# First projection of a two-layer decoder trunk: transposes of the normalised heads issued two half-products later, and the block sums of the second round's left operand formed when its rows are transposed

## Chip, cores and metric

The kernel runs on one core of a Trainium2 chip. The metric is device time in microseconds, the median of three runs. One more execution was taken by the hardware profiler, and all rows of the trace come from it. The engines are called as the profile calls them: PE (matmuls and transposes), PEld (its weight loads), DVE, ACT, POOL, and SP, which in this kernel issues every DMA.

## What is computed

The whole reference is two decoder layers over 2048 positions of width 1024. Only the first step of the first layer matters here: a row-wise RMS norm of x, one projection h @ w_in whose columns are cut into heads, and an RMS norm of the query and key heads of the forgetting attention.

```python
def even_layer(x, g_norm, w_in, b_f, g_q, g_k, w_out):
    h = rmsnorm(x, g_norm)
    proj = h @ w_in
    fq, fk, fv, f_logit, sq, sk, sv, gate = jnp.split(proj, split_points(EVEN_SIZES), axis=-1)
    ...
    fq = rmsnorm(split_heads(fq, N_FOX_HEADS, DENSE_HEAD_DIM), g_q)
    fk = rmsnorm(split_heads(fk, N_FOX_HEADS, DENSE_HEAD_DIM), g_k)
    fox = forgetting_attention(fq, fk, split_heads(fv, N_FOX_HEADS, DENSE_HEAD_DIM), log_f)
```

## The kernel before

The order of the program is: the first projection (`even_projection`, up to about 720 us), the attentions of the first layer, its output projection, and the second layer. Only the first projection is edited.

**Products.** Each fp32 operand is split into a high part (rounded by ACT, line 81) and the remainder (a subtraction on DVE or POOL, line 86), and each product is three matmuls (lines 91 to 93). A panel is 512 output columns for 1024 rows of x. It is computed by a Strassen-like scheme: the left operand (rows of x, transposed) and the weights are 2 by 2 block matrices, seven products A11, S2, A12, S3, S1, A22, S4 (line 177) take the place of eight, and each product is issued as two half-products. A half-product ends with a call of `tick()`, line 292. Four results come out of each panel, after the products A12, S1, A22 and S4; a result is two tiles `c` of 128x512 from the pool tag `res`, which has four buffers. `Weights.prepare` (lines 219 to 245) forms the sums of the weight blocks on POOL (line 226) and splits them into the tiles `wop`.

**Rounds and panels.** The 2048 rows are two rounds of 1024. Each round runs through the panels sq, sk, sv, fv, fk, fq, g0, g1 (line 708). In round 0 the first three are interleaved with the preparation of the left operand straight from x (`left_direct`).

**Heads of fk and fq.** The function `qk_fox` (line 629) takes a result of two tiles, squares them on ACT into tiles `sq` of the tag `c` (line 123; that tag has four buffers), reduces on DVE (line 124), takes an inverse root by short operations on DVE and ACT (lines 104 to 114), scales the tile (line 637), transposes it on PE (line 642), splits it (lines 77, 78) and stores it (line 647). All of this is issued in the program right behind the product.

**Left operand of round 1.** While round 0 runs fv and fk, rows 1024 to 2047 of x are loaded in eight tiles, normalised, transposed and stored to the DRAM array `hT0` (`transpose_to`, line 153, its transposes in line 142 and its copies into tiles `te`, tag `c`, in line 149). The jobs are started at line 743 and advance one step at every second half-product, three tiles in flight (`Pace`, `staggered`). In the last panel of round 0, g1, `left` (line 342) makes the seven blocks: it reloads `hT0` (two loads of 1 MB into `stage`, 16 of 256 KB into `lp`), forms the sums S2, S3, S1, S4 with 20 additions and subtractions of 128x512, half on DVE and half on POOL (line 345), and splits the 28 pieces (ACT line 81, DVE line 86). It advances one step after each product of g1.

**Order.** The order on each engine isn't the order of the program. A scheduler that works on a modelled timeline fixes it ahead of the run: each engine takes, among what is ready by its model, what stands first in the program. Each engine then works off its list in order.

Of the kernel before, what the change touches and what calls it, by code (L numbers as in the profile page):

```python
# [8 lines left out]
F32 = mybir.dt.float32  # L9
F32R = mybir.dt.float32r  # L10
BF = mybir.dt.bfloat16
AF = mybir.ActivationFunctionType
OP = mybir.AluOpType
# [4 lines left out]
P = 128  # L18
S = 2048
D = 1024  # L20
KT = D // P
CH = 512
NCH = S // CH
TPC = CH // P
NTT = S // P
# [11 lines left out]
class K:  # L37
# [114 lines left out]

    def transpose_to(self, T, src, t, gain):

        nc = self.nc
        x = self.w4([P, D], name="xt")
        nc.sync.dma_start(x, src[t * P:(t + 1) * P, :])
        yield
        self.normalise(x)
        yield  # L160
        self.transposed(x, gain, lambda z: self.c2([P, 4, P], name="te"),
                        lambda z, d: nc.sync.dma_start(T[:, z * 4:(z + 1) * 4, t * P:(t + 1) * P], d))

# [12 lines left out]
A11, A12, S2, S3, S1, A22, S4 = range(7)  # L176
ORDER = (A11, S2, A12, S3, S1, A22, S4)
FIRST = (A11, A12, S2, S3, S1, A22, S4)
# [77 lines left out]
def panel(*args, **kw):  # L256
    for _ in panel_steps(*args, **kw):
        pass
# [82 lines left out]

def left(k, T, r, A, staged=True):

# [15 lines left out]
    def piece(block, kk):  # L359
        c = k.c2(name="lp", tag=next(tags))  # L360
        t0 = r * ROUND + block * CH
        nc.sync.dma_start(c, T[:, kk, t0:t0 + CH])
        return c

    half = lambda t, kk: [t[:, kk, z].bitcast(F32) for z in range(2)]
    if staged:
        F = k.big([P, KT, CH], name="stage")
        for z in range(2):
            nc.sync.dma_start(F[:, z * 4:(z + 1) * 4], T[:, z * 4:(z + 1) * 4, r * ROUND:r * ROUND + CH])
    for z, name in enumerate(("A11", "A12")):  # L370
# [48 lines left out]
    yield  # L419


def left_direct(k, x, gain, A, spare):

    nc = k.nc
    sub, plus = OP.subtract, OP.add  # L430
    tt = lambda o, a, b, op, e=None: (e or nc.vector).tensor_tensor(o, a, b, op=op)
    xa, xb = (k.big([P, TPC, D], name=n) for n in ("xa", "xb"))
    tiles = [xa[:, t] for t in range(TPC)] + [xb[:, t] for t in range(TPC)]

    def load(ts):
        for t in ts:
            nc.sync.dma_start(tiles[t], x[t * P:(t + 1) * P, :])

    load(range(1))
    gb = k.w4([P, D], name="gb")  # L440
    nc.sync.dma_start(gb, gain.to_broadcast([P, D]))
    load(range(1, TPC))
    yield
    load(range(TPC, 2 * TPC))
    fa, fb = (k.big([P, KT, CH], name=n) for n in ("fa", "fb"))
    spare.extend(fb[:, j].bitcast(F32R) for j in range(4, KT))
    A.extend([None] * 7)
    new = lambda *js: [A.__setitem__(j, k.big([P, 4, 2, CH], F32R, name=f"A{j}")) for j in js]
    new(A11, A12, S2, A22)
    roots = {}  # L450

    def squares(*ts):
        ss = k.small.tile([P, 8], F32, name="ssx", tag="ss4")
        for j, t in enumerate(ts):
            nc.scalar.activation(k.c2([P, D], BF, name="junk"), tiles[t], AF.Square, accum_out=ss[:, j:j + 1])
        r = k.rstd(ss, 8, D, len(ts))
        for j, t in enumerate(ts):
            roots[t] = r[:, j:j + 1]

    def scaled(t):  # L460
        nc.vector.scalar_tensor_tensor(tiles[t], tiles[t], roots[t], gb, op0=OP.mult, op1=OP.mult)

    def transposed(t):
        pts = []
        for z in range(2):
            pt = k.ps("t" if z else "s")
            for j in range(4):
                c = z * 4 + j
                nc.tensor.transpose(pt[:, j * P:(j + 1) * P], tiles[t][:, c * P:(c + 1) * P], k.ident)
            pts.append(pt.rearrange("p (a b) -> p a b", a=4))  # L470
        return pts

    def put(j, i, src):
        k.split(A[j][:, :, 0, i], A[j][:, :, 1, i], src, "act", "dve")

    squares(0)
    ahead = {0: (1,), 1: (2, 3), 3: (4, 5), 5: (6, 7)}
    for t in range(2 * TPC):
        scaled(t)
        if t in ahead:  # L480
            squares(*ahead[t])
        i = slice(t % TPC * P, (t % TPC + 1) * P)
        p0, p1 = transposed(t)
        if t < TPC:
            for z, j in enumerate((A11, A12)):
                put(j, i, (p0, p1)[z])
                nc.scalar.activation(fa[:, z * 4:(z + 1) * 4, i], (p0, p1)[z], AF.Copy)
            if t == TPC - 1:
                yield
            continue  # L490
        a, s1 = fa[:, :4, i], fb[:, :4, i]
        nc.scalar.activation(s1, p0, AF.Copy)
        tt(a, a, p0, sub)
        s = k.c2([P, 4, P], name="s2")
        tt(s, p1, a, sub)
        put(S2, i, s)
        put(A22, i, p1)
        tt(s1, p1, s1, plus)
        tt(fa[:, 4:, i], fa[:, 4:, i], s, sub, nc.gpsimd)
        yield  # L500
    for j, src in ((S3, fa[:, :4]), (S1, fb[:, :4]), (S4, fa[:, 4:])):
        new(j)
        for kk in range(4):
            k.split(A[j][:, kk, 0], A[j][:, kk, 1], src[:, kk], "act", "dve")
        yield
# [88 lines left out]
def staggered(gens):  # L594

    gens, flight = iter(gens), []
    while True:
        flight = [g for g in flight if next(g, "end") != "end"]
        g = next(gens, None)
        if g is not None:  # L600
            next(g)
            flight.insert(0, g)
        elif not flight:
            return
        yield


def even_projection(k, x, w, first, first_left, early, late):
    tc, nc = k.tc, k.nc
    c2, dr = k.c2, k.dram  # L610
    k.fT = {n: dr.tile([P, 4, 2, S], F32R, name=f"f{n}T") for n in "qk"}
    k.sT = {n: dr.tile([P, 4, 2, S], F32R, name=f"s{n}T") for n in "qk"}
# [1 line left out]
    k.gT = dr.tile([P, 8, S], F32, name="gT")  # L614
    k.ncum = dr.tile([4, S], F32, name="ncum")
    k.mixT = dr.tile([P, 8, S], F32, name="mixT")
    T = dr.tile([P, KT, S], F32, name="hT0")
    y = k.consts.tile([P, 4, 32], F32, name="y")
    nc.gpsimd.memset(y, 0.0)
    r = 0  # L620
    ring, turn = [None], [0]

    def spare():
        turn[0] += 1
        return ring[0][turn[0] % len(ring[0])]
# [3 lines left out]
    def qk_fox(dst, gain):  # L629
        def emit(block, half, cs):  # L630
            rs = k.norms(cs, 4, P)
            for g, src in enumerate(cs):
                one(block, half, g, src, rs[:, g])

        def one(block, half, g, src, rs):
            qn = src.rearrange("p (a b) -> p a b", a=4)
            nc.vector.tensor_tensor(qn, qn, rs.unsqueeze(2).to_broadcast([P, 4, P]), op=OP.mult)
            pt = k.ps("t")
            for pr in range(2):
                for h in range(2):  # L640
                    c = (h * 2 + pr) * P
                    nc.tensor.transpose(pt[:, c:c + P], qn[:, pr * 2 + h], k.ident)
            hl = [spare(), spare()]
            k.split(hl[0], hl[1], pt, scale=getattr(k, gain))
            t0 = at(block, g, 256)
            for z in range(2):
                nc.sync.dma_start(dst[:, half * 2:half * 2 + 2, z, t0:t0 + 256].bitcast(F32),
                                  hl[z].rearrange("p (h t) -> p h t", h=2).bitcast(F32))
        return emit

    def value(dst, logits=False):
# [32 lines left out]
    def forget():  # L684
# [26 lines left out]
        ("sv", plain(2564), "t", value(k.v["s"])),  # L711
        ("fv", [[(1024, 256), (1536, 2)], [(1280, 256), (1538, 2)]], "t", value(k.v["f"], True)),
        ("fk", plain(512), "t", qk_fox(k.fT["k"], "gk")),
        ("fq", plain(0), "t", qk_fox(k.fT["q"], "gq")),
        ("g0", plain(3076), "d", gate(0)),
        ("g1", plain(3588), "d", gate(4)),
    ]
    W = Weights(k, [(w, seg) for _ in range(2) for _, seg, _, _ in kinds], [3] + [1] * 13)
    W.ahead(1)
    next(first)  # L720
    A = first_left
# [4 lines left out]
    tags = ("u", "x", "x")  # L726
# [4 lines left out]
    pace.finish()  # L731
    tick = Pace()
    tick.every = 2
    for r in range(2):
        B = []
        nxt = left(k, T, 1, B)
        box = k.big([P, KT, CH], F32R, name="ring")
        ring[0] = [box[:, j] for j in range(KT)]
        if r == 1:
            k.table()  # L740
        for n, (name, seg, mode, emit) in enumerate(kinds):
            if r == 0 and name == "fv":
                tick.add(staggered(k.transpose_to(T, x, t, k.ge) for t in range(TPC * 2, NTT)))
            if r == 0 and n < len(opened):
                next(opened[n], None)
                continue
            last = r == 0 and name == "g1"
            panel(k, A, W, mode, emit, tick, (lambda j: next(nxt)) if last else None,
                  258 if name == "fv" else 256)
            if r == 1 and name == "fv":  # L750
                forget()
        A = B
# [622 lines left out]
```

## Time and profile before

| | |
|---|---|
| median of 3 runs | 2784.57 us (2783.5 to 2787.73) |
| the profiled execution | 2782.93 us, of which the span from first to last instruction is 2781.2 us |
| busy in the span | PE 96%, DVE 70%, ACT 57%, POOL 40% |
| chain that ended last | PE 72%, DVE 17%, ACT 4%, DMA 3% |
| hT0 stores and reloads | 16 of 256 KB; 2 of 1 MB and 16 of 256 KB |

The page's busy share of PE is made of matmuls that overlap in a pipeline, so it hides lost time; the number of matmuls that start in a stretch shows it better. The view by windows gives both, for any stretch, together with the granted clock of PE. The view of waits says whose end an idle engine waited for. Rows of the timeline are: start, duration, engine, line, operation, output and inputs, count, and in brackets the idle time before it.

### The profile page before, as it was taken

What the parts mean: (1) busy time and instruction counts of PE and PEld (TensorE: products, weight loads), DVE (VectorE), ACT (ScalarE), POOL (GpSimd) and SP (SyncE); (2) the same over time, 40 slices, a digit from 0 to 9 for tenths busy, and PEclk for the clock granted to TensorE, in tenths of its full rate; (3) what the DMA queues carried; (4) which work ended last, traced back from release to release, by engine and by line L of the source; (5) the groups of instructions that cost most, each with busy time, mean ns of one, the idle gap of its engine ahead of it and who ended that gap; (6) DMA issues with size and microseconds to landing.
All of it is one profiled execution on the core that took longest, in us unless ns stands there. A gap on an engine that the chain in (4) does not pass through costs nothing.

```text
span 2781.2 us, 53979 instructions
## 1 busy us (share of the span) xinstructions
PE 2672.4 (96%) x19615; PEld 2423.1 (87%) x19615; DVE 1935.3 (70%) x4257; ACT 1579.9 (57%) x3843; POOL 1105.8 (40%) x905
## 2 busy tenths in 40 slices
PE   6999999999999999999999999999989999999998
PEld 5898878998777789988889899999879999999876
DVE  7857685675788887787337757475896685763966
ACT  6465454444776675666546335555664678665642
POOL 3545465444444443322004544353255432422322
PEclk9999999999999999999999999999999999999999
DMA  5577544545533334443664343344634454444675
GB/s 183 177 216 233 185 138 162 175 130 186 167 116 115 97 113 136 152 126 125 203 194 140 110 130 111 126 132 136 197 97 141 128 155 151 136 140 139 224 257 182
DMA packets 375146, 428.36 MB, mean 154 GB/s; under 512 B 30624, under 2 KB 309472, under 8 KB 374880
## 3 DMA queue, kind: packets, MB, share of 16 engines
q1 hardware_dynamic: 374880, 424.91, 47.9%
q8 instruction: 155, 2.54, 0.4%
q14 instruction: 111, 0.91, 0.1%
HBM read 270.25 MB, written 154.57 MB: 153 GB/s over the span
## 4 chain that ended last, share of the span: by engine, by line
PE 72%; DVE 17%; ACT 4%; DMA 3%; issue 2%; POOL 1%; SPq 0%; DVEq 0%; ACTq 0%; POOLq 0%
PE ps L91 20%; PE ps L93 20%; PE ps L92 19%; DVE rest L828 4%; PE ps L863 3%; PE ps L1172 2%; PE ps L1162 2%; PE ps L1143 2%; DVE pT L86 1%; PE ps L1088 1%; DVE wop L86 1%; DVE A L86 1%; DVE lp L345 1%; DVE c L300 1%; PE ps L1135 1%
## 5 line engine op out<-in xcount | busy, mean ns | idle before, releaser
L226 POOL TENSOR_TENSOR wraw<-wraw 128x512 f32<-128x512 f32 (+1 forms) x288 | 396.4, 1387 | 422.6 <-DVE wop L86 156.1
L81 ACT ACTIVATE wop<-wraw 128x512 fp32r<-128x512 f32 (+1 forms) x504 | 316.3, 631 | 351.4 <-PE ps L93 281.8
L86 POOL TENSOR_TENSOR wop<-wraw,wop 128x512 fp32r<-128x512 f32 (+1 forms) x216 | 290.6, 1348 | 504.4 <-ACT wop L81 490.9
L91 PE MATMUL ps<-wop,A 128*128 128x256 f32 (+1 forms) x1600 | 456.2, 286 | 4.1 <-DVE c L300 3.0
L92 PE MATMUL ps<-wop,A 128*128 128x256 f32 (+1 forms) x1600 | 455.9, 285 | 0.0
L93 PE MATMUL ps<-wop,A 128*128 128x256 f32 (+1 forms) x1600 | 453.7, 284 | 0.0
L91 PE MATMUL ps<-wop,S 128*128 128x256 f32 (+1 forms) x1536 | 442.3, 288 | 4.1 <-DVE c L300 4.1
L92 PE MATMUL ps<-wop,S 128*128 128x256 f32 (+1 forms) x1536 | 437.4, 285 | 2.4 <-DVE wop L86 2.4
L93 PE MATMUL ps<-wop,S 128*128 128x256 f32 (+1 forms) x1536 | 438.1, 285 | 0.0
L86 DVE TENSOR_TENSOR wop<-wraw,wop 128x512 fp32r<-128x512 f32 (+1 forms) x288 | 236.6, 822 | 233.1 <-ACT wop L81 228.4
L91 PEld LDWEIGHTS ps<-wop,A 128*128 128x128 f32 x1600 | 303.6, 190 | 8.5 <-DVE c L300 3.5
L93 PEld LDWEIGHTS ps<-wop,A 128*128 128x128 f32 x1600 | 304.5, 190 | 1.4 <-issue 0.8
L92 PEld LDWEIGHTS ps<-wop,A 128*128 128x128 f32 x1600 | 304.5, 190 | 1.2 <-issue 0.5
L91 PEld LDWEIGHTS ps<-wop,S 128*128 128x128 f32 x1536 | 291.2, 190 | 8.4 <-issue 5.9
L92 PEld LDWEIGHTS ps<-wop,S 128*128 128x128 f32 x1536 | 291.7, 190 | 4.1 <-DVE wop L86 2.6
L93 PEld LDWEIGHTS ps<-wop,S 128*128 128x128 f32 x1536 | 291.7, 190 | 3.2 <-issue 2.6
L81 ACT ACTIVATE pT<-ps 128x512 fp32r<-128x512 f32 (+2 forms) x352 | 165.0, 503 | 136.9 <-PE ps L863 93.4
L300 DVE TENSOR_TENSOR c<-u,ps 128x512 f32<-128x512 f32 (+1 forms) x242 | 157.4, 656 | 90.4 <-PE ps L93 83.6
L86 DVE TENSOR_TENSOR pT<-ps,pT 128x512 fp32r<-128x512 f32 (+2 forms) x352 | 187.8, 559 | 44.2 <-ACT pT L81 42.6
L831 POOL TENSOR_TENSOR rows<-rows,rest 128x512 f32<-128x512 f32 (+4 forms) x160 | 152.6, 957 | 160.2 <-DVE rest L828 152.4
L1155 ACT ACTIVATE row<-row,nm 128x256 f32<-128x256 f32 (+1 forms) x384 | 172.7, 453 | 63.7 <-DVE nm L1153 63.2
L92 PE MATMUL ps<-pT,vt 128*128 128x256 f32 x576 | 171.2, 299 | 7.7 <-DVE pT L86 5.9
(224 smaller groups left out, 6806.4 us busy)
## 6 DMA issues: line engine op xcount, KB each, us to landing
wraw<-in_odd_w_in_dram SPq DMA_DIRECT2D x88, 512.0 KB, 3.9
wraw<-in_even_w_in_dram SPq DMA_DIRECT2D x70, 512.0 KB, 4.3
ld<-qk SPq DMA_DIRECT2D x106, 256.0 KB, 3.2
qk<-c SPq DMA_DIRECT2D x96, 256.0 KB, 2.5
lp<-hT SPq DMA_DIRECT2D x60, 256.0 KB, 3.5
uu<-ot SPq DMA_DIRECT2D x96, 132.0 KB, 1.8
fin<-uu SPq DMA_DIRECT2D x16, 792.0 KB, 4.7
xt<-in_x_dram SPq DMA_DIRECT2D x24, 512.0 KB, 4.5
```

The source lines that it names most:

```text
L81: nc.scalar.activation(hi, src, AF.Copy)
L86: (nc.vector if lo_on == "dve" else nc.gpsimd).tensor_tensor(lo, src, hi.bitcast(F32), op=OP.subtract)
L91: mm(out, a[0], b[0], start=start, stop=False, skip_group_check=more)
L92: mm(out, a[0], b[1], start=False, stop=False, skip_group_check=more)
L93: mm(out, a[1], b[0], start=False, stop=stop, skip_group_check=more)
L226: tt = lambda e, o, x, y, op, s: e.tensor_tensor(o[:, s], x[:, s], y[:, s], op=op)
L300: nc.vector.tensor_tensor(out[g], x[g], y[g], op=OP.add)
L828: nc.vector.tensor_tensor_scan(o[:, b:b + n][:, ::-1], back, k.ident[:, :1].to_broadcast([P, n]), 1.0 if carry is None else carry, OP.mult ...
L831: nc.gpsimd.tensor_tensor(dst[:, :w], dst[:, :w], o[:, b + 1:b + 1 + w], op=OP.mult)
L863: nc.tensor.transpose(pt[:, (jx * 2 + i) * P:(jx * 2 + i + 1) * P], rows[:, i, (jj * 2 + jx) * P:(jj * 2 + jx + 1) * P], k.ident)
L1143: nc.tensor.matmul(scores(hp, e), q[pr, za, hp], ring[pr, zb, hp, blocks], start=i == 0, stop=i == 2)
L1155: nc.scalar.activation(row[:, h // 2, h % 2, :nk], row[:, h // 2, h % 2, :nk], AF.Exp, bias=nm[:, h:h + 1], accum_out=ot[:, HW + HG + h:HW ...
```

## The change

Two edits, both in the first projection.

In `qk_fox` the norm and the scaling stay where they were, behind the product. The transposes, the split and the stores go into a list `delayed`, and the new `later()`, which is called with every half-product (`beat` takes the place of `tick`), issues them at the second call, that is behind both halves of the next product.

For round 1, `transpose_to` and `left` are replaced. `combined_to` takes two tiles of x at a time, i of rows 1024 to 1535 and i of rows 1536 to 2047, transposes both into four tiles `te`, forms the four sums S1, S2, S3, S4 there (two operations on POOL, two on DVE, each 128x512), and stores all seven blocks into a DRAM array `U`. There are four such jobs, one after the other, each of six steps, so 24 steps at one per product, from fv into g0. `left_ready`, in g1, only loads the 28 pieces of `U` and splits them. `tick.finish()` ahead of g1 issues what is left of the jobs.

```diff
+def combined_to(U, k, src, ta, tb, i, gain):
+    nc = k.nc
+    xs = {}
+    for t in (ta, tb):
+        xs[t] = k.w4([P, D], name="xt")
+        nc.sync.dma_start(xs[t], src[t * P:(t + 1) * P, :])
+    yield
+    for t in (ta, tb):
+        k.normalise(xs[t])
+        yield
+    got = {}
+    def store(j, d):
+        nc.sync.dma_start(U[:, j, :, i * P:(i + 1) * P], d)
+    for t in (ta, tb):
+        k.transposed(xs[t], gain, lambda z: got.setdefault((t, z), k.c2([P, 4, P], name="te")))
+        yield
+    a0, a1, b0, b1 = got[ta, 0], got[ta, 1], got[tb, 0], got[tb, 1]
+    store(A11, a0)
+    store(A12, a1)
+    store(A22, b1)
+    s1, s2, s4 = (k.c2([P, 4, P], name="lp", tag=n) for n in ("ld", "q", "pT"))
+    nc.gpsimd.tensor_tensor(s1, b0, b1, op=OP.add)
+    store(S1, s1)
+    nc.vector.tensor_tensor(s2, s1, a0, op=OP.subtract)
+    store(S2, s2)
+    nc.gpsimd.tensor_tensor(b0, a0, b0, op=OP.subtract)
+    store(S3, b0)
+    nc.vector.tensor_tensor(s4, a1, s2, op=OP.subtract)
+    store(S4, s4)
+    yield
+def left_ready(k, U, A, tags):
+    A.extend([None] * 7)
+    tags = itertools.cycle(tags)
+    for j in FIRST:
+        t = A[j] = k.big([P, 4, 2, CH], F32R, name=f"A{j}")
+        for kk in range(4):
+            c = k.c2(name="lp", tag=next(tags))
+            k.nc.sync.dma_start(c, U[:, j, kk])
+            k.split(t[:, kk, 0], t[:, kk, 1], c, "act", "dve")
+        yield
...
-    T = dr.tile([P, KT, S], F32, name="hT0")
+    U = dr.tile([P, 7, 4, CH], F32, name="hU")
+    delayed = []
+    def later():
+        for pause, work in list(delayed):
+            if next(pause, None) is None:
+                next(work)
+                delayed.pop(0)
...
             for g, src in enumerate(cs):
-                one(block, half, g, src, rs[:, g])
-        def one(block, half, g, src, rs):
-            qn = src.rearrange("p (a b) -> p a b", a=4)
-            nc.vector.tensor_tensor(qn, qn, rs.unsqueeze(2).to_broadcast([P, 4, P]), op=OP.mult)
+                qn = src.rearrange("p (a b) -> p a b", a=4)
+                nc.vector.tensor_tensor(qn, qn, rs[:, g].unsqueeze(2).to_broadcast([P, 4, P]), op=OP.mult)
+                delayed.append((iter("-"), one(block, half, g, qn)))
+        def one(block, half, g, qn):
             pt = k.ps("t")
...
+    def beat():
+        later()
+        tick()
     for r in range(2):
-        nxt = left(k, T, 1, B)
+        nxt = left_ready(k, U, B, ("c", "c", "ld", "q", "pT"))
...
-                tick.add(staggered(k.transpose_to(T, x, t, k.ge) for t in range(TPC * 2, NTT)))
+                tick.add(*[combined_to(U, k, x, 8 + i, 12 + i, i, k.ge) for i in range(4)])
...
-            panel(k, A, W, mode, emit, tick, (lambda j: next(nxt)) if last else None,
+            if last:
+                tick.finish()
+            panel(k, A, W, mode, emit, beat, (lambda j: next(nxt)) if last else None,
```

More of the change, by code (lines that the diff above doesn't have):

```diff
@@ L648, in one @@
                                   hl[z].rearrange("p (h t) -> p h t", h=2).bitcast(F32))
+            yield
         return emit
```

## The prediction

> **What bounds the kernel now.** I read the page first.
>
> ```profile
> span 2781.2 us, 53979 instructions
> PE 2672.4 (96%) x19615; PEld 2423.1 (87%) x19615; DVE 1935.3 (70%) x4257; ACT 1579.9 (57%) x3843; POOL 1105.8 (40%) x905
> ```
> PE is busy 96% of the span, so the end moves only by PE time that is lost, and the first projection (to about 720 us) is to be searched for it. The view by windows shows the last panel of round 0, g1:
>
> ```profile
> 360.00:380.00 20.00, 15.39 (x58) 11.52 (x57) 20.00 (x17) 9.03 (x18) 15.87 (x10) 0.91 0.55 170
> 380.00:400.00 20.00, 18.32 (x78) 14.00 (x76) 19.47 (x25) 13.74 (x25) 10.81 (x8) 1.00 0.51 172
> 400.00:420.00 20.00, 19.82 (x86) 15.76 (x86) 10.80 (x14) 8.73 (x16) 11.73 (x9) 1.00 0.41 132
> 420.00:440.00 20.00, 20.00 (x88) 16.15 (x87) 12.59 (x15) 8.42 (x14) 13.70 (x10) 1.00 0.51 184
> ```
> The numbers behind PE are matmul starts. An undisturbed 20 us holds 88 of these 512-wide matmuls; the three stretches ahead hold 58, 78 and 86. That is 30 + 10 + 2 = 42 too few, 42/88 x 20 = **9.5 us lost in g1**.
>
> For fk and fq I compare rounds: the copy of the first product of fk and that of g0 stand two panels apart, in round 0 and in round 1.
>
> ```profile
> 211.88 1.18 ACT L305 ACTIVATE u<-ps 128x512 f32<-128x512 f32 x2
> 306.18 0.60 ACT L305 ACTIVATE u<-ps 128x512 f32<-128x512 f32 x1 [0.41 <-PE ps L93]
> 554.09 0.60 ACT L305 ACTIVATE u<-ps 128x512 f32<-128x512 f32 x1 [0.79 <-PE ps L93]
> 639.44 0.60 ACT L305 ACTIVATE u<-ps 128x512 f32<-128x512 f32 x1 [0.42 <-PE ps L93]
> ```
> ```profile
> 212.00:308.00 96.00, 3.16 (x24) 2.66 (x24) 0.96 0.63 206
> ```
> Round 0 takes 306.18 - 211.88 = 94.30 us, round 1 takes 85.35 us with no wait of PE. Of the 8.95 us, 24 transposes of x, which only round 0 has, take at most 3.16 us, so about **5.8 us are lost in fk and fq**. The waits of PE, first from 176 to 312 us, then from 340 to 410 us:
>
> ```profile
> PE ps L642 <- DVE c L637: 5.0, 4, 2.8
> PE ps L91 <- ACT wop L81: 1.0, 1, 1.0
> PE ps L142 <- ACT xt L133: 0.7, 1, 0.7
> ```
> ```profile
> PE ps L93 <- DVE wop L86: 4.8, 3, 3.5
> PE ps L91 <- ACT wop L81: 1.4, 1, 1.4
> ```
> So the fk and fq loss is PE waiting for the scaled heads, the **fv** panel loses 1.0 + 0.7 = 1.7 us beside the x tiles, and g1 waits for split weights, most of it for DVE. All that can be won is 9.5 + 5.8 + 1.7 = 17.0 us. More is lost than waited, because the clock falls after a gap:
>
> ```profile
> 264.00:268.00 4.00, 1.18 (x10) 0.98 (x9) 4.00 (x6) 0.36 (x1) 4.00 (x4) 0.95 0.00 0
> 268.00:272.00 4.00, 3.85 (x17) 3.56 (x18) 4.00 (x6) 1.47 (x3) 1.08 (x1) 0.50 0.21 70
> 276.00:280.00 4.00, 4.00 (x36) 4.00 (x35) 2.12 (x4) 2.81 (x5) 0.00 (x0) 1.00 1.00 302
> ```
> The third stretch is the full rate, 36 starts in 4 us; after the gap of 2.8 us the clock is 0.50 and 17 start.
>
> **Why DVE is late in g1.** POOL and DVE, same time:
>
> ```profile
> 365.71 5.12 POOL L345 TENSOR_TENSOR stage<-stage,lp 128x512 f32<-128x512 f32 x3
> 370.79 3.40 POOL L86 TENSOR_TENSOR wop<-wraw,wop 128x512 fp32r<-128x512 f32 x2
> 366.22 5.15 DVE L86 TENSOR_TENSOR S<-lp,S 128x512 fp32r<-128x512 f32 x3
> 371.30 1.75 DVE L86 TENSOR_TENSOR wop<-wraw,wop 128x512 fp32r<-128x512 f32 x1
> 387.46 0.68 DVE L86 TENSOR_TENSOR wop<-wraw,wop 128x512 fp32r<-128x512 f32 x1
> ```
> The same DVE split of weights takes 0.68 us with POOL idle and 1.75 us beside POOL's L345. So two-input operations on the two engines nearly take turns: the sums of the left operand slow the weight splits twice, as instructions in DVE's list and as POOL work beside it.
>
> **The change, part by part.**
>
> *Removed from g1:* the sums. Grouped from 340 to 402 us:
>
> ```profile
> L345 POOL TENSOR_TENSOR stage<-stage,lp 128x512 f32<-128x512 f32 x6 | 10.3, 1724 | 1.2 <-DVE A L86 1.2
> L345 POOL TENSOR_TENSOR lp<-lp 128x512 f32<-128x512 f32 x3 | 5.3, 1776 | 1.6 <-DMA lp<-hT 1.6
> L345 DVE TENSOR_TENSOR lp<-lp 128x512 f32<-128x512 f32 x2 | 3.5, 1769 | 0.0
> L345 DVE TENSOR_TENSOR lp<-lp,stage 128x512 f32<-128x512 f32 x1 | 1.8, 1767 | 0.0
> L345 DVE TENSOR_TENSOR stage<-stage,lp 128x512 f32<-128x512 f32 x2 | 1.4, 680 | 0.0
> ```
> That is 15.6 us of POOL and 6.7 us of DVE. The 28 pieces are still split on ACT and DVE.
>
> ```profile
> 340.00:402.00 62.00, 55.54 (x227) 42.96 (x226) 53.97 (x55) 36.49 (x64) 41.58 (x28) 0.97 0.41 132
> 552.00:642.00 90.00, 90.00 (x735) 88.69 (x734) 72.10 (x126) 44.70 (x88) 38.88 (x31) 1.00 0.40 126
> ```
> DVE was busy 53.97 of 62 us there; without 6.7 us it is 47.3, or 76%, and with 9 POOL operations fewer beside it less still. In round 1, fk and fq run DVE at 72.10 of 90 us, 80%, and lose nothing. So g1 could recover all 9.5 us. The other end is nothing, if the loads become the limit. I take 7.5, near the first end, because 80% without loss is the nearest row, and leave 2 for bursts.
>
> *Added ahead of g1:* 16 sums of 128x512, 8 on DVE and 8 on POOL, in four jobs, where 10 and 10 stood. Two jobs fall into fk and fq (steps 7 to 18 of 24). The normalisations of x are the same eight, but four of them now come in fk and fq, and the transposes and their ACT copies go with them. DVE's need there, on top of round 1's 72.10 in 90 us: 4 sums at 0.68 to 1.75 us, 2.7 to 7.0; 4 POOL sums, each holding up at most one DVE operation by 1.75 - 0.68, 0 to 4.3; 4 x 5 short root operations. Their duration is seen in these rows:
>
> ```profile
> 222.45 0.58 ACT L305 ACTIVATE c<-ps 128x512 f32<-128x512 f32 x1
> 236.88 1.20 ACT L123 ACTIVATE sq<-c 128x512 f32<-128x512 f32 x2
> 244.10 1.22 DVE L112 TENSOR_SCALAR t<-t 128x8 f32<-128x8 f32 x1
> 249.59 0.17 DVE L112 TENSOR_SCALAR t<-t 128x8 f32<-128x8 f32 x1
> 251.21 1.28 DVE L300 TENSOR_TENSOR c<-u,ps 128x512 f32<-128x512 f32 x2
> ```
> The same L112 takes 0.17 us, or 1.22 us behind POOL; twenty of them take 3.4 to 24.4 us. DVE's sum is 78.2 to 107.8 of 90 us. I take sums at 1.75, POOL's 4.3 and 0.3 us per short operation, nearest to the uncontended row since the x tiles are spread thinly: 89.4 us, just full. The loss in fk and fq now comes from a pile-up in fk: a result copied at 222.45 has its squares only at 236.88, because the copies of x tiles fill ACT and the four buffers of tag `c`; results queue, and an addition that reads the banks runs only at 251.21. One x tile per three products in place of one per product thins that out. Between all 5.8 us won and as much lost again, I take 2 won. In fv the tiles thin out likewise; of 1.7 I take 1.0.
>
> *Transposes later.* In round 1 a result is copied and transposed at
>
> ```profile
> 565.84 0.60 ACT L305 ACTIVATE c<-ps 128x512 f32<-128x512 f32 x1 [0.75 <-PE ps L93]
> 575.73 0.60 PE L642 MATMUL ps<-ident,c 128*128 128x128 f32 x4
> ```
> 9.9 us apart. Two half-products are 85.35/28 x 2 = 6.1 us. The order on PE already puts the transposes later than the edit demands, because the model has the heads ready no sooner, so the edit moves little: I take 0. If it does add slack, it wins the 5.0 us of the L642 waits; if it holds the `res` tiles longer, it costs as much as one such wait, 2.8 us. Behind a delayed transpose on PE nothing else is held that isn't held today.
>
> *DMAs.* Stores go from 16 to 28 of 256 KB, loads from 2 of 1 MB and 16 of 256 KB to 28 of 256 KB: 4 MB more in all, on one SP list.
>
> ```profile
> hT<-te SPq DMA_DIRECT2D x16, 256.0 KB, 4.7
> lp<-hT SPq DMA_DIRECT2D x16, 256.0 KB, 4.1
> ```
> Stores of S1 to S4 wait for POOL and DVE, and weight loads stand behind them in SP's list; four weight buffers cover that. A late load costs POOL's L226, then the weight split, then PE. I take 0: the old stores ran at one tile per product, the new at less than one per two products. In g1, 7 MB of loads against 4 MB; the DMA share there was 0.41, and 7/4 of all of it would be 0.72. What isn't hidden lands in g1's left-over 2 us.
>
> *Sum.* 7.5 + 2 + 1 = 10.5 us. The profiled span 2781.2 becomes 2770.7, with the 1.7 us around it (2782.93 - 2781.2) 2772.4; the median lies 1.6 us above the profiled execution: **2774.0 us**. About 0.2%, 5.6 us, can be told from no change, so faster means under 2779.0, slower over 2790.1.
>
> **The rivals.**
>
> *B, everything clears.* All 17.0 us: 2767.6. For it: round 1 runs the same panels without loss. Against it: round 0 still has the x tiles, and 28 splits in g1.
>
> *C, the work only moves.* If short operations on DVE meet POOL's sums half of the time, 0.7 us each, DVE's sum in fk and fq is 97.4 of 90 us, 7.4 us over; with the bursts kept, that pays back g1's 7.5: 2784.5. For it: L112 at 1.22 us. Against it: the x tiles' short operations run while POOL works a minority of the time, 38.88 of 90 us.
> The Trainium skill, SBUF — State Buffer, section "Who interferes with whom", states the mechanism: a DVE operation with two SBUF inputs and a GpSimd operation that reads SBUF exclude each other for the whole instruction. The rows 0.68 and 1.75 us agree. By that rule alone the lock time of the sums is carried into fuller panels, and C is its forecast.
>
> *D, slower: tag `c` becomes the bound.* A job holds all four `c` buffers from its second transposition until the sums are done and stored: 2 x 1.72 + 2 x 1.77 + 4.7 = 11.7 us. The squares of the heads need the same tag. A head chain of 9.9 us becomes 21.6; its `res` tiles are needed again three products later, 85.35/14 x 3 = 18.3 us. So PE would lose 3.3 us and some 2 us of clock (17 starts for 36 in 4 us) in each of fk and fq, 10.6 us more than now; and in g1 twelve of the 28 loads share the tag with the eight gate tiles, so g1 recovers nothing: 2784.57 + 10.6 = 2795. It decides once a job holds the tag over 18.3 - 9.9 = 8.4 us. Against it: the second job's hold starts in fk before a product without a result, and uncontended sums, 0.68 us on DVE, shorten it.
>
> *The change doesn't do what it says*: for the first edit that is my forecast.
>
> **How the numbers follow.** The forecast 0.50, with a range of its own from 2768 (fk and fq clear too) to 2779; B 0.16; C 0.23; D 0.11. Faster: the forecast and B, 0.66; same: C, 0.23; slower: D, 0.11. The range reaches from 2764, B with the later schedule falling out some us better, to 2788, past C; D is left out.
>
> **What would show it.** From 360 to 420 us of the old timeline, matmul starts near 88 per 20 us, no L345, and weight splits of DVE nearer 0.68 than 1.75 us. Two panels fk and fq in 89 to 93 us. L642 still some 9 to 10 us behind the copy in round 1. Wrong would be: PE waits for L637 over 8 us, squares over 14 us behind their copies in fq (D), DVE full through fk, fq and g0 (C), or PE waiting in g1 or early in round 1 for pieces of the left operand.

## The result, and the profile after

| | before | after |
|---|---|---|
| median | 2784.03 us, 4 runs | 2768.63 us, 4 runs |
| span of the profiled execution | 2781.2 us | 2766.0 us |

The ratio is 0.9949 with a 95% interval from 0.9938 to 0.9961: faster by 0.5%, some 14 to 15 us where 10.5 were forecast. From the page of the kernel after:

```profile
span 2766.0 us, 54039 instructions
PE 2664.9 (96%) x19615; PEld 2418.7 (87%) x19615; DVE 1923.3 (70%) x4255; ACT 1577.2 (57%) x3843; POOL 1102.5 (40%) x903
```
PE's work is the same (19615 instructions); its busy share says as little as before. The view by windows, the stretches of g1 that were shown of the kernel before:

```profile
360.00:380.00 20.00, 20.00 (x88) 16.24 (x87) 17.54 (x21) 12.30 (x22) 8.61 (x6) 1.00 0.88 285
380.00:400.00 20.00, 19.68 (x85) 15.42 (x84) 11.63 (x14) 11.63 (x19) 12.43 (x11) 1.00 0.28 89
400.00:420.00 20.00, 20.00 (x88) 16.21 (x87) 13.93 (x17) 8.01 (x13) 10.65 (x7) 1.00 0.73 264
420.00:440.00 20.00, 20.00 (x88) 16.23 (x87) 6.27 (x10) 7.75 (x13) 10.12 (x8) 1.00 0.37 113
```
Starts are 88, 85, 88, 88 where they were 58, 78, 86, 88: the hole in g1 is gone. The waits of PE from 176 to 312 us, then from 312 to 412 us:

```profile
PE ps L699 <- DVE c L691: 4.0, 4, 1.5
PE ps L91 <- DVE c L300: 0.2, 1, 0.2
```
```profile
PE ps L91 <- DVE c L300: 0.3, 1, 0.3
```
No wait for split weights is left in g1. The waits for the scaled heads (L699, L691 are the old L642, L637) are 4.0 us, where they were 5.0.

Where the time went is read from the copy of the first product of each panel. First the kernel before (fv, g1, and sk of round 1; fk and g0 were shown in the prediction), then the kernel after (fv, fk, g0, g1, sk of round 1):

```profile
160.14 0.39 ACT L305 ACTIVATE u<-ps 128x258 f32<-128x258 f32 x1 [1.47 <-PE ps L93]
346.88 0.60 ACT L305 ACTIVATE u<-ps 128x512 f32<-128x512 f32 x1 [0.72 <-PE ps L93]
434.59 0.60 ACT L305 ACTIVATE u<-ps 128x512 f32<-128x512 f32 x1 [0.72 <-PE ps L93]
```
```profile
159.59 0.39 ACT L305 ACTIVATE u<-ps 128x258 f32<-128x258 f32 x1 [1.48 <-PE ps L93]
208.09 1.06 ACT L305 ACTIVATE u<-ps 128x512 f32<-128x512 f32 x2
299.27 0.59 ACT L305 ACTIVATE u<-ps 128x512 f32<-128x512 f32 x1
341.43 0.60 ACT L305 ACTIVATE u<-ps 128x512 f32<-128x512 f32 x1 [0.72 <-PE ps L93]
420.08 0.60 ACT L305 ACTIVATE u<-ps 128x512 f32<-128x512 f32 x1 [0.72 <-PE ps L93]
```

| stretch | before, us | after, us | difference |
|---|---|---|---|
| fv | 51.74 | 48.50 | -3.2 |
| fk and fq | 94.30 | 91.18 | -3.1 |
| g0 | 40.70 | 42.16 | +1.5 |
| g1 and the panel sq after it | 87.71 | 78.65 | -9.1 |
| the four | 274.45 | 260.49 | -14.0 |

The rest of the 15.2 us between the two spans, 1.2 us, lies ahead of fv (0.55) and behind the panel sq (0.69), where both kernels run through the same lists of instructions; nothing shows a cause for it. Part of the table is only a move: the transposes of x, by panel (fv, then fk and fq, then g0), in the kernel before, then in the kernel after:

```profile
161.00:212.00 51.00, 5.50 (x40) 4.56 (x40) 1.00 0.72 221
212.00:306.00 94.00, 3.16 (x24) 2.66 (x24) 0.96 0.64 210
306.00:347.00 41.00, 0.00 (x0) 0.00 (x0) 1.00 0.62 205
```
```profile
160.00:208.00 48.00, 2.24 (x16) 1.83 (x16) 1.00 0.69 213
208.00:299.00 91.00, 5.02 (x32) 4.43 (x32) 0.98 0.59 186
299.00:341.00 42.00, 2.07 (x16) 1.83 (x16) 1.00 0.98 331
```
40, 24 and 0 transposes became 16, 32 and 16. At 2.07/16 = 0.13 us each, 3.1 us of PE work left fv, 1.0 went to fk and fq and 2.1 to g0. Without it, fv won about 0.1, fk and fq 4.1, g0 0.6. These are rough, since the busy time of a pipelined transpose overlaps its neighbours: in the timeline eight of them set PE back by about 0.8 us, which makes fv's own win 0.8, that of fk and fq 3.9, and g0's 0.1.

### The profile page after: what moved, and what is told of

Same layout as the page of the kernel before. It is cut to its first block, busy times and chain, and to the rows that moved or that the text cites. A ratio compares the mean times of both kernels' runs of the same rounds, so it can differ in the third digit from the quotient of the medians.

```text
span 2766.0 us, 54039 instructions
## 1 busy us (share of the span) xinstructions
PE 2664.9 (96%) x19615; PEld 2418.7 (87%) x19615; DVE 1923.3 (70%) x4255; ACT 1577.2 (57%) x3843; POOL 1102.5 (40%) x903
## 4 chain that ended last, share of the span: by engine, by line
PE 70%; DVE 17%; ACT 5%; DMA 3%; issue 3%; POOL 1%; SPq 1%; DVEq 0%; ACTq 0%; POOLq 0%
PE ps L91 19%; PE ps L93 19%; PE ps L92 19%; DVE rest L893 4%; PE ps L928 3%; PE ps L1237 2%; PE ps L1227 2%; PE ps L1208 2%; PE ps L1153 1%; DVE pT L86 1%; DVE wop L86 1%; DVE c L300 1%; DVE row L1214 1%; PE ps L1200 1%; DVE lp L345 1%
## 5 line engine op out<-in xcount | busy, mean ns | idle before, releaser
L91 PE MATMUL ps<-wop,A 128*128 128x256 f32 (+1 forms) x1856 | 528.5, 285 | 3.8 <-DVE c L300 3.8
L92 PE MATMUL ps<-wop,A 128*128 128x256 f32 (+1 forms) x1856 | 527.2, 284 | 0.0
L93 PE MATMUL ps<-wop,A 128*128 128x256 f32 (+1 forms) x1856 | 525.5, 283 | 0.0
L86 POOL TENSOR_TENSOR wop<-wraw,wop 128x512 fp32r<-128x512 f32 (+1 forms) x216 | 291.2, 1351 | 494.4 <-ACT wop L81 479.5
L86 DVE TENSOR_TENSOR wop<-wraw,wop 128x512 fp32r<-128x512 f32 (+1 forms) x288 | 234.1, 814 | 239.8 <-ACT wop L81 237.6
L91 PE MATMUL ps<-wop,S 128*128 128x256 f32 x1280 | 369.8, 289 | 4.5 <-DVE c L300 4.5
L92 PE MATMUL ps<-wop,S 128*128 128x256 f32 x1280 | 364.1, 284 | 2.4 <-DVE wop L86 2.4
L93 PE MATMUL ps<-wop,S 128*128 128x256 f32 x1280 | 365.6, 286 | 0.0
L91 PEld LDWEIGHTS ps<-wop,A 128*128 128x128 f32 x1856 | 351.9, 190 | 8.1 <-DVE c L300 4.6
L93 PEld LDWEIGHTS ps<-wop,A 128*128 128x128 f32 x1856 | 352.3, 190 | 1.2 <-issue 0.7
L92 PEld LDWEIGHTS ps<-wop,A 128*128 128x128 f32 x1856 | 352.0, 190 | 0.7 <-issue 0.5
L91 PEld LDWEIGHTS ps<-wop,S 128*128 128x128 f32 x1280 | 242.6, 190 | 8.8 <-issue 8.0
L92 PEld LDWEIGHTS ps<-wop,S 128*128 128x128 f32 x1280 | 243.1, 190 | 4.2 <-DVE wop L86 2.6
L93 PEld LDWEIGHTS ps<-wop,S 128*128 128x128 f32 x1280 | 242.8, 190 | 3.4 <-issue 2.7
L300 DVE TENSOR_TENSOR c<-u,ps 128x512 f32<-128x512 f32 (+1 forms) x242 | 157.4, 656 | 90.3 <-PE ps L93 84.6
L86 DVE TENSOR_TENSOR pT<-ps,pT 128x512 fp32r<-128x512 f32 (+2 forms) x352 | 187.7, 559 | 43.8 <-ACT pT L81 42.3
L93 PE MATMUL ps<-A,wop 128*128 128x512 f32 x448 | 177.2, 397 | 4.4 <-DVE ms L104 4.4
```

What stands on the lines that cost most here:

```text
L86: (nc.vector if lo_on == "dve" else nc.gpsimd).tensor_tensor(lo, src, hi.bitcast(F32), op=OP.subtract)
L91: mm(out, a[0], b[0], start=start, stop=False, skip_group_check=more)
L92: mm(out, a[0], b[1], start=False, stop=False, skip_group_check=more)
L93: mm(out, a[1], b[0], start=False, stop=stop, skip_group_check=more)
L300: nc.vector.tensor_tensor(out[g], x[g], y[g], op=OP.add)
```

## The experiments

**First edit alone**, on the kernel before:

```diff
-                one(block, half, g, src, rs[:, g])
+                delayed.append((iter("-"), one(block, half, g, qn)))
...
+    def beat():
+        later()
+        tick()
```

> The kernel before with only the first edit: transposes of the normalised heads two half-products later. My theory: the model already places these transposes later than the edit asks, so the order on every engine stays and the time is that of before, 2784 us within 2 us, with the waits of PE for the scaled heads still at about 5.0 us. Rival: the edit gives slack and wins those waits and the clock behind them, 2776 to 2780 us.

Measured: ratio 0.9998 (0.9989 to 1.0006), no change. The lists of instructions of all five engines are the same, row by row, as those of the kernel before. This is what the theory expected: alone, the edit does nothing, and PE's waits for the scaled heads stay (4.6 us). The gain comes with the second edit; the second edit without the first was not run.

**Sums left out of g1**, on the kernel before:

```diff
-        nxt = left(k, T, 1, B)
+        nxt = left(k, T, 1, B, sums=False)
```

> The kernel before, whose left() leaves out the 20 sums of the left operand in g1 (so S2, S3, S1 and S4 of round 1 hold unsummed blocks); loads, stage and the 28 splits stay. Theory that the sums make the weight splits late: the 9.5 us lost in g1 fall to 2 or less, the time is 2774 to 2778 us. Rival that the order of the buffers (stage takes the first free one, so the blocks come a product late) makes them late: g1 still loses over 6 us, 2780 to 2784 us.

Measured: 0.9964 (0.9951 to 0.9977). The copies at the start of g1 and of sk:

```profile
347.63 0.60 ACT L305 ACTIVATE u<-ps 128x512 f32<-128x512 f32 x1 [0.72 <-PE ps L93]
425.52 0.60 ACT L305 ACTIVATE u<-ps 128x512 f32<-128x512 f32 x1 [0.72 <-PE ps L93]
```
77.89 us, where the kernel before takes 87.71 and the kernel after 78.65. The sums, 20 operations, cost 9.8 us of PE there. The loads, `stage` and the buffers stayed, so the rival that their order makes the splits late is out. PE waited for nothing from 312 to 412 us.

**Sums put back into g1**, on the kernel after:

```diff
             k.nc.sync.dma_start(c, U[:, j, kk])
+            if j not in (A11, A12):
+                (k.nc.gpsimd if kk % 2 else k.nc.vector).tensor_tensor(c, c, c, op=OP.add)
```

> The kernel after, with 20 additions of 128x512 put back into g1, 10 on DVE and 10 on POOL, one for each piece of S2, S3, S1, A22 and S4 (so these pieces of round 1 are doubled). The sums at the transposes stay. Theory that DVE and POOL with two SBUF inputs take turns and so delay the weight splits: g1 loses 5 to 9.5 us again, 2774 to 2778 us. Rival that the buffers' order made the gain: within 2 us of 2768.6.

Measured: 0.9974 (0.9963 to 0.9985), where the kernel after has 0.9949. The same two copies:

```profile
339.59 0.60 ACT L305 ACTIVATE u<-ps 128x512 f32<-128x512 f32 x1 [0.38 <-PE ps L93]
426.63 0.60 ACT L305 ACTIVATE u<-ps 128x512 f32<-128x512 f32 x1 [0.72 <-PE ps L93]
```
87.04 us: 8.4 of the 9.1 us are back, as the theory expected, though the median of 2779.75 us lies just above its 2774 to 2778. PE's list is that of the kernel after, so no other order on PE makes the difference. But the way to PE is another one than in the kernel before. Its waits from 312 to 412 us:

```profile
PE ps L91 <- DVE c L300: 2.6, 2, 1.9
PE ps L91 <- DVE u L300: 2.5, 2, 1.8
```
PE doesn't wait for split weights here, but for the additions with which DVE empties the banks (L300). So what the sums make late is DVE as a whole; which of its operations PE waits for differs between the two kernels.

**Which half of the sums.** The kernel before with only DVE's ten, and with only POOL's ten:

```diff
-    tt = lambda o, a, b, op, e=None: (e or nc.vector).tensor_tensor(o, a, b, op=op)
+    tt = lambda ...: ... if not only or e is None else None       # the other kernel: e is not None
```

> The kernel before, whose left() keeps the ten sums of DVE in g1 and leaves out POOL's ten (so the blocks that POOL summed stay unsummed). From the start of g1 to the second panel of round 1 the kernel before takes 87.7 us, without any sums 77.9, so the sums cost 9.8. If the cost lies in turn-taking with POOL, leaving out POOL's sums wins most of it, 78 to 81 us; if it lies in DVE's own list, little: 84 to 87 us.

> The kernel before, whose left() keeps POOL's ten sums and leaves out DVE's ten (blocks unsummed accordingly). If turn-taking with POOL is the cost, the same stretch stays at 84 to 87 us; if DVE's own list is, it falls to 78 to 81 us. If both are needed to overload DVE, both runs fall to about 80.

Measured: 0.9968 (0.9958 to 0.9977) and 0.9993 (0.9983 to 1.0004). The two copies, with DVE's sums only, then with POOL's only:

```profile
346.01 0.60 ACT L305 ACTIVATE u<-ps 128x512 f32<-128x512 f32 x1 [0.72 <-PE ps L93]
424.13 0.60 ACT L305 ACTIVATE u<-ps 128x512 f32<-128x512 f32 x1 [0.72 <-PE ps L93]
```
```profile
345.35 0.60 ACT L305 ACTIVATE u<-ps 128x512 f32<-128x512 f32 x1 [0.72 <-PE ps L93]
427.71 0.60 ACT L305 ACTIVATE u<-ps 128x512 f32<-128x512 f32 x1 [0.72 <-PE ps L93]
```
78.12 us and 82.36 us. The first is where turn-taking put it (78 to 81); the second lies between the two expectations, and both together come nearest to the third reading, that both halves are needed. Leaving out POOL's ten wins 9.6 of the 9.8 us; leaving out DVE's ten wins 5.3. Put the other way, DVE's ten alone cost 0.2 us, POOL's ten alone 4.5, and both together 9.8. So it is not the length of DVE's list alone: POOL's sums are the larger part, and DVE's ten matter only beside them. With DVE's sums only, PE waits for nothing from 312 to 412 us; with POOL's only, it waits for

```profile
PE ps L93 <- DVE wop L86: 1.1, 2, 0.9
PE ps L93 <- POOL wop L86: 1.1, 1, 1.1
PE ps L91 <- ACT wop L81: 1.0, 1, 1.0
```
So POOL's sums reach PE by two ways: they hold up DVE's weight splits, and POOL's own weight splits stand behind them in its list. In the kernel before the first is by far the larger: 4.8 us of PE's waits there are for DVE's weight splits. The whole times of the two runs hold other changes too: the lists of DVE and POOL also differ near 1420 and from 1960 to 2040 us.

The weight splits on DVE in the stretch of g1, kernel before (340 to 402 us), then the kernel after (335 to 398 us) with its pieces' splits:

```profile
L86 DVE TENSOR_TENSOR wop<-wraw,wop 128x512 fp32r<-128x512 f32 x10 | 11.8, 1175 | 3.4 <-ACT wop L81 3.3
```
```profile
L86 DVE TENSOR_TENSOR wop<-wraw,wop 128x512 fp32r<-128x512 f32 x12 | 9.8, 825 | 9.0 <-ACT wop L81 9.0
L86 DVE TENSOR_TENSOR A<-lp,A 128x512 fp32r<-128x512 f32 x26 | 26.8, 1069 | 4.7 <-ACT A L81 4.7
```
The mean weight split falls from 1175 to 825 ns; the pieces' splits, at 1069 ns, still meet POOL's weight work and are simply not late any more. The Trainium skill, SBUF — State Buffer, section "Who interferes with whom", has DVE and GpSimd exclude each other for a whole instruction when the DVE operation has two SBUF inputs and the GpSimd operation reads SBUF. These runs agree with it: a weight split on DVE takes 0.68 us with POOL idle and 1.75 beside an operation of POOL (the prediction's rows), and on the mean 825 ns where POOL's sums are gone.

**x tiles thinned out, sums left in g1**, on the kernel before:

```diff
-                tick.add(staggered(k.transpose_to(T, x, t, k.ge) for t in range(TPC * 2, NTT)))
+                tick.add(*[k.transpose_to(T, x, t, k.ge) for t in range(TPC * 2, NTT)])
```

> The kernel before, with its eight x tiles transposed one after the other, one per two products, in place of one per product with three in flight; sums stay in g1. Theory that the thinning, not the moved sums, won the 6 us in fv, fk and fq: fv to the start of g0 takes 4 to 6 us less, g1 still loses about 9, the time is 2778 to 2780 us. Rival that the thinning does nothing and the win there is an accident of the new order, or comes from the early sums that left: 2782 to 2785 us.

Measured: slower, 1.0034 (1.0022 to 1.0045), which neither side had. The panels say something else: fv 48.07, fk and fq 93.49, g0 42.54, g1 and sq 87.80. From fv to the start of g0 that is 4.5 us less than the kernel before, as the theory had it, and g1 loses as before; but g0 takes 1.8 us more, so 2.6 us are left. Most of the loss, over 10 us, is in the last 180 us, in which nothing was edited. Two stretches of the kernel before, then the same of this one:

```profile
2600.00:2620.00 20.00, 19.39 (x164) 16.76 (x162) 19.77 (x58) 11.75 (x33) 5.96 (x5) 1.00 0.66 212
2700.00:2720.00 20.00, 20.00 (x142) 16.15 (x141) 16.70 (x54) 10.40 (x34) 6.30 (x5) 1.00 0.69 247
```
```profile
2600.00:2620.00 20.00, 19.39 (x173) 17.06 (x172) 19.90 (x55) 11.51 (x32) 6.62 (x5) 1.00 0.58 182
2700.00:2720.00 20.00, 16.92 (x111) 13.31 (x109) 12.45 (x48) 8.81 (x30) 4.38 (x4) 0.95 0.66 221
```
From 2600 to 2620 us both start about as many instructions on PE; from 2700 to 2720 us 142 become 111, and the span is 2794.4 us. The lists differ there: with its early work shifted, the scheduler's model orders parts of the second layer and of the last step another way. In the kernel after it doesn't: behind g1, its lists are those of the kernel before. So thinning alone wins 2.6 of the 4.9 us that the kernel after wins from fv to g0, hardly more than three executions of one list differ by there (2.4 us), and a whole time can't be put down to the panel that was edited without looking at the rest.

**x tiles as dense as the pace allows**, on the kernel after:

```diff
-    tick.every = 2
+    tick.every = 1
```

> The kernel after with the jobs advanced at every half-product in place of every second one, so all 24 steps fall into fv and the first products of fk. Theory that spreading the x tiles wins in fv and costs in g0: fv to the start of fk goes back up by 2 to 3.5 us to about 51, g0 comes down by 1 to 2 us to about 41, g1 stays near 44; the time is 2768 to 2772 us. Rival that the density doesn't matter: every panel within 1 us of the kernel after. If the four buffers of tag c held by a job are what costs, fk loses 5 us or more and the time is over 2774.

Measured: 0.9998 (0.999 to 1.0007): the whole gain is gone. The copies of fv, fk and fq, and the waits of PE from 176 to 312 us:

```profile
158.85 0.39 ACT L305 ACTIVATE u<-ps 128x258 f32<-128x258 f32 x1 [1.48 <-PE ps L93]
217.71 0.57 ACT L305 ACTIVATE u<-ps 128x512 f32<-128x512 f32 x1
267.37 0.58 ACT L305 ACTIVATE u<-ps 128x512 f32<-128x512 f32 x1
```
```profile
PE ps L142 <- ACT xt L133: 5.2, 2, 3.0
PE ps L91 <- ACT u L305: 4.2, 1, 4.2
PE ps L91 <- DVE c L300: 2.9, 3, 1.4
```
fv takes 58.86 us (48.50 in the kernel after) and fk 49.66 (43.52); g1 and sq take 77.09, a little better still. PE waits for x tiles that ACT hasn't scaled and for banks that ACT and DVE haven't emptied. At twice the pace the jobs, which hold two x tiles and four `te` at once, cost what the move of the sums wins; paces between the two were not run. The expectation was too small, 2 to 3.5 us in fv; the rival of tag `c` had the size right for fk, but the waits name ACT's chain of the x tiles first, and the two weren't separated.

**A longer delay of the transposes**, on the kernel after, four and three half-products:

```diff
-                delayed.append((iter("-"), one(block, half, g, qn)))
+                delayed.append((iter("---"), one(block, half, g, qn)))       # "--" for three
```

> The kernel after with the transposes of the heads four half-products later in place of two (12.2 us, more than the 9 to 10 us at which the model places them). Theory that the edit was only too short to change the order: the 4.0 us of waits for the scaled heads in fk and fq, and the clock behind them, go: 3 to 6 us less, 2763 to 2766 us. Rival that the results' four buffers, held longer, stop PE instead: waits of PE for L300 appear and the time is 2768 to 2775 us.

> The kernel after with the transposes three half-products later (9.1 us, about where the model places them). If a longer delay helps by the slack it gives, half of what four give: 2765 to 2768 us. If results held longer cost, nothing to lose yet: within 1 us of the kernel after.

Measured: 0.9973 (0.9963 to 0.9982) for four, 0.9941 (0.9928 to 0.9955) for three. Three is no different from two. Four costs some 7 us by the ratios, and the waits that it was to remove are still there, 4.7 us from 176 to 312 us where 4.0 stood. Instead g0 takes 46.43 us, and fq of round 1 takes 49.27 (copies of fq and g0, and PE's wait from 410 to 680 us):

```profile
583.80 0.58 ACT L305 ACTIVATE u<-ps 128x512 f32<-128x512 f32 x1
633.07 0.58 ACT L305 ACTIVATE u<-ps 128x512 f32<-128x512 f32 x1
```
```profile
PE ps L699 <- DVE c L691: 4.1, 2, 3.0
```
In round 1 of the kernel after fq takes 43.25 us with no such wait. The slack turned into late work behind it, but not as the rival said: the waits are for the scaled heads (L691). Waits for L300 show only in g1 (2.0 us, at 377 and 384 us), long behind the last transposes of round 0's heads, so results held longer don't explain them.

**All sums at the transposes on DVE**, on the kernel after:

```diff
-    nc.gpsimd.tensor_tensor(s1, b0, b1, op=OP.add)
+    nc.vector.tensor_tensor(s1, b0, b1, op=OP.add)
...
-    nc.gpsimd.tensor_tensor(b0, a0, b0, op=OP.subtract)
+    nc.vector.tensor_tensor(b0, a0, b0, op=OP.subtract)
```

> The kernel after with all 16 sums at the transposes on DVE, none on POOL. Theory that POOL's sums hold DVE's short operations up in fk and fq: the waits for the scaled heads fall below 4.0 us and fk and fq take 1 to 2 us less; 2766 to 2768 us. Rival that DVE's own list is the limit there: fk and fq take 1 to 3 us more, 2769 to 2772 us.

Measured: 0.9944 (0.9932 to 0.9957), fk and fq 91.59 us for 91.18. The waits for the scaled heads are 4.6 us, not below 4.0. No difference that can be told: whether two sums per job run on POOL or on DVE does not matter where the jobs are spread. Neither side of the expectation. What all the sums together cost there is not shown, since no run leaves them out.

**Both kernels profiled again:**

> The kernel before, profiled once more: fk and fq together took 94.30 us in its first profile and 92.07 in that of the first edit alone, whose lists are the same. Expected between 91.5 and 94.5 us; it tells how much of the 3.1 us between before and after in these panels is spread between executions.

> The kernel after, profiled once more: fk and fq together took 91.18 us. Expected between 89.5 and 92.5 us; if it lies above the lowest of the kernel before, the win in fk and fq isn't told from none. fv within 0.5 us of 48.50, g1 to the second panel of round 1 within 1 us of 78.65.

Measured: fk and fq 93.87 us before, 91.34 after; with the first edit's run, three executions of the same lists give 94.30, 92.07 and 93.87. The kernel after gives 91.18 and 91.34, and the run with the sums put back into g1, whose lists are the same up to there, 89.98 (copies at 207.45 and 297.43). The means of the threes differ by 2.6 us, the nearest two by 0.7: a win there is likely, its size isn't settled. fv 52.25 and 48.40; g1 and sq 87.79 and 78.75: these hold within 0.5 and 0.1 us.

## Why the prediction was right

The forecast was 10.5 us faster, 2774.0; it is some 14 to 15 us, 2768.6, inside the range and faster as the likeliest case said. It lies only 0.6 us inside the forecast's own 2768 to 2779. Of the 4.7 us between 10.5 and the 15.2 by which the spans differ, g1 has 1.6, fk and fq 1.1, fv and g0 together 0.7, and 1.2 lie outside the four stretches.

- **g1, 7.5 us taken, 9.1 measured.** Right in place, and in the main in mechanism; the 2 us kept back for bursts weren't needed. The bound of 9.5 from counted starts was nearly reached, and leaving all sums out gives 9.8. One reading was wrong: the weight split of 1.75 us at 371.30 stands beside POOL's own weight splits (370.79, L86), not beside its sums. Those splits are still there in the kernel after, so the mean weight split fell to 825 ns, not to 680. And late weight splits on DVE are not the only way in which such sums stop PE, as the runs with the sums put back and with POOL's sums alone show.
- **fk and fq, 2 us taken, 3.1 measured, 2.6 on the means.** The size came out nearly, its working did not. DVE's need there was put at 89.4 of 90 us; the row of the kernel after (208 to 299 us), and of the same panels in round 1 (540 to 625 us), says

```profile
208.00:299.00 91.00, 88.08 (x708) 85.98 (x708) 71.29 (x134) 56.26 (x130) 55.26 (x52) 0.98 0.59 186
540.00:625.00 85.00, 85.00 (x703) 84.11 (x702) 67.65 (x118) 41.33 (x80) 36.06 (x28) 1.00 0.40 127
```
71.29 of 91 us, some 18 us less. What was added to round 1's figure was too high: 17.3 us for sums, hold-ups by POOL's sums and short operations, where these two rows differ by 3.6. That round 1's figure already holds the contention with POOL's weight work is a likely reason, but is not shown. The pile-up in fk that the prediction named is gone:

```profile
214.97 0.60 ACT L305 ACTIVATE c<-ps 128x512 f32<-128x512 f32 x1 [0.76 <-PE ps L93]
219.42 1.21 ACT L123 ACTIVATE sq<-c 128x512 f32<-128x512 f32 x2
```
The squares of the first result start 4.5 us behind its copy, where 14.4 stood. It was worth little: on the means of three executions fk takes 0.9 us less, and fq, where no such pile-up stood, 1.7. So what makes fk and fq better is still not shown; that the jobs must be thin there is (dense, fk takes 6 us more).
- **fv, 1.0 taken, 3.2 measured.** The term missed that a moved transpose takes its PE time along: 24 of them left fv, and 16 came to g0, where 1.5 us are lost that were put at nothing. The transposes are a move, and without them fv's own win is 0.1 to 0.8, near the 1.0 at best.
- **First edit, 0 taken:** shown on the kernel before. The distance of 9.9 us between copy and transposes against 6.1 us asked was the right sign to read; in round 1 of the kernel after, copy and transposes still stand 9.9 us apart (551.09 and 560.95).
- **DMAs, 0 taken:** no wait of PE shows a load of U; agrees.
- **Rival B**, 17.0 us and 2767.6, was nearer than the forecast: g1 cleared nearly whole, fk and fq about half. **Rival C**, that the work only moves, failed: it had DVE 7.4 us over in fk and fq, and DVE is busy for 71.29 of 91 us there. **Rival D** asked that a job hold tag `c` for over 8.4 us from its second tile's copies on; in fq of the kernel after, these copies and the next square on ACT stand at

```profile
268.43 2.17 ACT L149 ACTIVATE te<-ps,ge 128x128 f32<-128x128 f32 x8
274.64 0.62 ACT L123 ACTIVATE sq<-c 128x512 f32<-128x512 f32 x1
```
so the square starts 6.2 us after the copies do (5.9 in fk, 229.60 to 235.46), under the 8.4. What D feared is there in small: this result was copied at 265.98, so its squares start 8.7 us behind, where the prediction called over 14 a sign of D.

## What to carry to other kernels

When a stage loses time because two engines take turns, look at the one off the path too: here POOL's ten sums cost PE 4.5 us alone and 9.6 beside DVE's ten, mostly by making DVE late, while DVE's ten alone cost almost nothing. Forming the sums elsewhere paid here only with the jobs that carry them spread thinly (at twice the pace the whole gain was gone). Before an edit that issues something later, read how far behind its input it already runs; if that is more than the edit asks, it may change nothing, as here. Where a scheduler orders the lists, compare the unedited stages too: one variant won 2.6 us where it was edited and lost over 10 in the last 180 us.

## What the runs showed of the hardware that was not expected

Executions of one program differ by more than three of them suggest: 19 runs of the kernel before on one chip lie between 2778.32 and 2789.49 us, and a pair of panels with the same lists takes between 92.07 and 94.30 us, while the same pair in round 1, where PE waits for nothing, repeats within 0.1 us (85.35, 85.35 and 85.34). So part of the spread sits where PE stops and waits, and a saving of 2 us there needs more than one profile. Where the rest of the 11 us lies is not shown.
